# A backbone layer with sparse experts: row transposes of two experts together, one branch an expert, and the last experts' tokens finished in slot order

## The chip, the cores and the metric

One core of one Trainium2 chip runs the kernel. The metric is the device time of one execution in microseconds (us); lower is better.

## What is computed

One layer: a token mixer, then a mixture of experts, on 512 latent tokens of 1024 channels, all float32. The change touches the experts and the final norm alone. For each token the router picks one group of eight experts and in it two experts:

```python
top_logits, top_idx = lax.top_k(in_group, TOP_K)
weights = jax.nn.softmax(top_logits, axis=-1) * p_group
expert_id = g_idx * EXPERTS_PER_GROUP + top_idx
for e in range(N_EXPERTS):
    act = jax.nn.silu(h @ w_gate[e]) * (h @ w_up[e])
    out = out + gate[:, e:e + 1] * (act @ w_down[e])
x = x + gt2 * out.reshape(x.shape)
return rmsnorm(x, g_final)
```

There are 32 experts; each has gate and up matrices of 1024 x 256 and a down matrix of 256 x 1024, so 3 MB of weights. Both experts of a token are in the same group.

## The kernel before, in words

The mixer and the router end with tables: for each expert the list of its tokens (`ix`, and `ixh` for halves of rows), the number of its tokens as a class of size (`size`), and the two weights of each token (`pw`). Normalised tokens lie in DRAM (`h2d`), the residual stream too (`x1d`).

**The loop (L1632 to L1673)** has 33 rounds. In round e TensorE multiplies expert e by gate and up and expert e - 1 by down:
- `gather_e` (L1397): GpSimd reads the size into a register, walks a tree of branches and gathers up to 128 rows of `h2d` by an indirect DMA into one of two tiles `xg`.
- `tile_x` (L1329): eight transposes bring the rows to channel-major in PSUM; ScalarE and VectorE copy four each to `st`.
- `tile_gu` (L1347): gate and up for 64 tokens. Two column halves of the array work on gate and up. A second half (tokens 65 to 128) runs under a branch in `halves` (L1408).
- `tile_act` (L1352) and `tile_at` (L1358): silu and product, four transposes of 64 x 64 out of partitions 64 to 127, one copy to `at`.
- `tile_down` (L1367), again with a second half under a branch.
- `tile_y` (L1376): VectorE multiplies by the gate of the residual branch; `scatter_e` (L1415) writes half rows to `ybuf` in DRAM, the second half under a branch of GpSimd.

So TensorE meets two branches an expert, and one register load `load_wide` (L1613). On TensorE, ScalarE and VectorE the order is as written; on GpSimd and the DMA queue of SyncE a scheduler orders by when it takes an instruction to be ready. Weights come through a ring of 20 buffers (`eraw`, `part_load`), some six experts ahead.

**The end.** Tokens of experts 30 and 31 are not scattered: `last_prepare` and `last_turn` build one-hot matrices, `last_y` splits the results into a high and a low part, and `last_own` adds them to the sum in PSUM by matmuls (L1580), where `last_x` (L1575) has put the residual rows and `last_mix` (L1587) adds the scattered results that `last_rows` (L1564) loads. Sum of squares, square root, reciprocal and the last product follow for four tiles of 128 tokens; each is stored by a plain DMA.

Of the kernel before, what the change touches and what calls it, by code (L numbers as in the profile page):

```python
# [26 lines left out]
def hybrid_kernel(  # L27
# [8 lines left out]
    nc = tc.nc  # L36
# [1213 lines left out]
    for c_ in range(2):  # L1250
        gcopy(gt2h[64 * c_:64 * c_ + 64], gt2[64 * c_:64 * c_ + 64, 512 * c_:512 * c_ + 512])
        G.memset(cofs[64 * c_:64 * c_ + 64], float(c_))
    xgs = [mo.tile([128, D], F32, name=f"xg{j}", tag=f"xg{j}", bufs=1) for j in range(NXG)]
    for a_ in xgs:
        G.memset(a_, 0.0)

    pw = mz2.tile([128, NT, 2], F32, name="pw")

# [41 lines left out]
    ix = indices(pt[:, 0:2 * NE].rearrange("p (a e) -> p a e", a=2), 128, NE, "tb")  # L1300
    pcnt = ps_s5("pcnt")
# [14 lines left out]
    V.tensor_tensor_scan(cnt[:, 3], onesf1, cnt[:, 2], 0.0, op0=ALU.mult, op1=ALU.add)  # L1316
    ngen = mz2.tile([1, 1], I32, name="ngen")
# [11 lines left out]
    def tile_x(xg, st, h):  # L1329

        pt = ps_tp("pxt").rearrange("p (k s) -> p k s", k=4)
        for k in range(4):
            T.transpose(pt[:, k, :], xg[:, 4 * h + k:D:8], ident)  # L1333
        if h:
            V.tensor_copy(st[:, 4:8], pt)  # L1335
        else:
            S.activation(st[:, 0:4], pt, AF.Copy)

    def new_st():
        return mo.tile([128, KD, 128], F32, tag="st", name="st")  # L1340
# [6 lines left out]
    def tile_gu(pg, st, r, a):  # L1347
        for k in range(KD):
            for c in range(2):
                T.matmul(pg[H[c], 256 * a:256 * a + 256], lhsT=st[:, k, H[a]], rhs=r[c][k // 4][:, 256 * (k % 4):256 * (k % 4) + 256], start=(k == 0), stop=(k == KD - 1), skip_group_check=True)  # L1350

    def tile_act(pg):  # L1352
        sg = mo.tile([128, 512], F32, tag="sge", name="sge", bufs=2)
        S.activation(sg[64:128], pg[0:64], AF.Silu)
        V.tensor_tensor(sg[64:128], pg[64:128], sg[64:128], op=ALU.mult)
        return sg

    def tile_at(sg):  # L1358
# [37 lines left out]

    def gather_e(e):  # L1397
        if e < NE:
            more[e] = nc.values_load(size[0:1, e:e + 1], engines=[EN.Pool], min_val=0, max_val=len(SIZES) - 1, skip_runtime_bounds_check_because=BYC)
            by_size(e, lambda n: gather(xgs[e % NXG][0:n], ix[0:n, 0, e:e + 1]))  # L1400

    scattered = []

    def scatter_h(e, a, y):
        return G.indirect_dma_start(out=ybuf.rearrange("r (c n) -> (r c) n", c=2), out_offset=bass.IndirectOffsetOnAxis(ap=ixh[:, a, e:e + 1], axis=0),  # L1405
                                    in_=y[:, 512 * a:512 * a + 512], in_offset=None, bounds_check=4 * L - 1, oob_is_err=False)
# [15 lines left out]

    for e in range(NXG):
        gather_e(e)

# [3 lines left out]
    with tc.If(n_gen > 0):  # L1429
        with tc.For_i(0, n_gen, 1):  # L1430
            row = mz2.tile([1, 3, NE], F32, name="grow")
# [44 lines left out]
            xt_ = new_st().rearrange("p k s -> p (k s)")  # L1476
# [18 lines left out]
            pd = [ps_mm("ped0"), ps_mm("ped1")]  # L1495
            for k in range(2):
# [9 lines left out]
    x1s = []  # L1506

    def last_loads():
        for h in range(2):
            t = eraw("x1").rearrange("p (i d) -> p i d", i=2)  # L1510
            SY.dma_start(out=t, in_=x1d[256 * h:256 * h + 256].rearrange("(i p) d -> p i d", p=128))
            x1s.append(t)
        x1s.append(eraw("gfin")[:, 0:1024])
        SY.dma_start(out=x1s[2], in_=g_final.rearrange("(o d) -> o d", o=1).to_broadcast([128, D]))


    DIRECT = (NE - 2, NE - 1)
    last = {}

    sel = mz2.tile([128, 2, 2, NT, 2], F32, name="sel")  # L1520

    def last_weights():

        for j, e in enumerate(DIRECT):
            V.tensor_scalar(sel[:, j, 0], ex, float(e), None, op0=ALU.is_equal)
            V.tensor_tensor(sel[:, j, 1], sel[:, j, 0], pw, op=ALU.mult)
            V.tensor_tensor(sel[:, j, 1, :, 0], sel[:, j, 1, :, 0], sel[:, j, 1, :, 1], op=ALU.add)

    def last_prepare(j):

        g, t = (xgs[j][:, 512 * k:512 * k + 512].rearrange("p (i s) -> p i s", i=NT) for k in range(2))
        gtt(g, oh[:, :, 0, :], sel[:, j, 0, :, 0:1].to_broadcast([128, NT, 128]), ALU.mult)
        gtt(t, oh[:, :, 1, :], sel[:, j, 0, :, 1:2].to_broadcast([128, NT, 128]), ALU.mult)
        gtt(g, g, t, ALU.add)

    def last_turn(j):
        if j == 0:
            last["oh"] = eraw("loh").bitcast(F32R)
            last["gs"] = mz2.tile([128, 2], F32, name="gs")
        pt = ps_tp("pht")  # L1540
        for i in range(NT):
            T.transpose(pt[:, 128 * i:128 * i + 128], xgs[j][:, 128 * i:128 * i + 128], ident)
        S.activation(last["oh"][:, 512 * j:512 * j + 512], pt, AF.Copy)
        pg = ps_tp("pgs")
        for i in range(NT):
            T.matmul(pg[:, 0:1], lhsT=xgs[j][:, 128 * i:128 * i + 128], rhs=sel[:, j, 1, i, 0:1], start=(i == 0), stop=(i == NT - 1))  # L1546
        V.tensor_copy(last["gs"][:, j:j + 1], pg[:, 0:1])

    def last_y(pd, j):

        y, parts = new_y(), eraw("yp").bitcast(F32R)
        g_ = last["gs"][:, j:j + 1]
        for a in range(2):
            for c in range(2):
                V.tensor_tensor(y[H[a], 512 * c:512 * c + 512], pd[a][H[c]], gt2h[H[c]], op=ALU.mult)  # L1555
        hi, lo = parts[:, 0:1024], parts[:, 1024:2048]
        S.activation(hi, y, AF.Copy, scale=g_)
        V.scalar_tensor_tensor(lo, y, g_, hi.bitcast(F32), op0=ALU.mult, op1=ALU.subtract)
        return hi, lo

    ssf = mz2.tile([128, 4, NT], F32, name="ssf")
    yrs, xis, fin = [], [], {}

    def last_rows():  # L1564

        for i in range(NT):
            t = eraw("yr").rearrange("p (q d) -> p q d", q=2)
            yb = bass.AP(ybuf.tensor, ybuf.offset + 128 * i * D, [[D, 128], [L * D, 2], [1, D]])
            ld = SY.dma_start(out=t, in_=yb)
            for p_ in scattered:  # L1570
                tc.add_manual_dep(ld.ins if hasattr(ld, "ins") else ld, (p_.ins if hasattr(p_, "ins") else p_).name, mybir.DependencyInfo(mybir.DependencyClass.Sync, mybir.DependencyReason.DATA), reason="results of every expert")
# [146 lines left out]
```

## Time and profile before

| | us |
|---|---|
| runs shown | 882.38, 878.52, 880.90 |
| median | 880.9 |
| profiled execution | 880.24 |
| its span, first to last instruction | 878.5 |
| TensorE busy in the span | 738.2 (84%) |
| VectorE, ScalarE, GpSimd busy | 458.5, 321.2, 329.6 |

The span is what the trace covers; the profiled execution's own time lies 1.7 us above it. Busy shares are means over stages: the experts' loop fills the stretch from about 552 to 850 us, and the end follows it. In rows of the trace PE is TensorE's multiplier, PEld its weight load, DVE VectorE, ACT ScalarE, POOL GpSimd; a q behind a name is that engine's sequencer.

### The profile page before, as it was taken

How to read it: one execution, taken by the hardware profiler on the slowest of the kernel's cores; microseconds unless marked ns; L12 is line 12 of the kernel's file. 1: busy time of each engine (PE TensorE's matmuls, PEld its weight loads, DVE VectorE, ACT ScalarE, POOL GpSimd, SP SyncE). 2: the span in 40 equal slices, each digit the busy share in tenths (PEclk: the TensorE clock that was granted, in tenths of full speed). 3: DMA queues.
4: the chain of work that ended last, by engine and by line, in shares of the span. 5: the costliest groups of instructions: out<-in, count | busy, mean ns of one | idle time of the engine just before them, and what ended most of it. 6: DMA issues, size and time to landing. Idle time of an engine off the chain costs nothing. (4 is left out here: it accounts for less than half of the span.)

```text
span 878.5 us, 14308 instructions
## 1 busy us (share of the span) xinstructions
PE 738.2 (84%) x5486; PEld 513.4 (58%) x5486; DVE 458.5 (52%) x723; ACT 321.2 (37%) x559; POOL 329.6 (38%) x293
## 2 busy tenths in 40 slices
PE   3498986998978986979999993788998998888885
PEld 0376863665656775746778872455655655555542
DVE  3948565355397798725985576133223232332344
ACT  3442621355465748526632331221112112121133
POOL 4647435345486697621610122122122122221400
PEclk9998997999989999989999996899999999999999
DMA  8916870342145454478687437999989998998042
GB/s 308 272 47 194 196 230 22 106 126 73 48 140 174 150 177 130 137 241 322 202 297 274 156 121 314 394 392 398 381 304 388 406 360 332 387 397 295 18 192 95
DMA packets 84679, 202.01 MB, mean 230 GB/s; under 512 B 12860, under 2 KB 42622, under 8 KB 74867
## 3 DMA queue, kind: packets, MB, share of 16 engines
q1 hardware_dynamic: 76754, 180.00, 57.7%
q0 software_dynamic: 5856, 12.45, 4.0%
q10 hardware_dynamic: 1984, 8.44, 3.6%
q8 instruction: 53, 0.87, 0.4%
q14 instruction: 32, 0.25, 0.1%
HBM read 180.16 MB, written 26.69 MB: 235 GB/s over the span
## 5 line engine op out<-in xcount | busy, mean ns | idle before, releaser
L1350 PE MATMUL peg<-eraw,st 128*64 128x256 f32 x1152 | 132.8, 384 | 8.4 <-PEq L1411 6.8
L1350 PEld LDWEIGHTS peg<-eraw,st 128*64 128x64 f32 x1152 | 94.1, 138 | 58.8 <-issue 33.9
L1335 DVE COPY st<-pxt 128x512 f32<-128x512 f32 x32 | 22.1, 691 | 158.7 <-PE pxt L1333 158.7
L1364 ACT ACTIVATE at<-pat 128x256 f32<-128x256 f32 x32 | 12.3, 383 | 216.0 <-PE pat L1362 216.0
L1322 POOL DMA_INDIRECT xg<-h2d,tb x32 | 30.3, 948 | 141.3 <-PE pxt L1333 129.9
L396 PE MATMUL zp<-hh,zuwh 128*128 128x512 f32 x192 | 78.2, 407 | 0.0
L398 PE MATMUL zp<-hh,zuwl 128*128 128x512 f32 x192 | 76.2, 397 | 0.5 <-POOL zuwl L757 0.4
L397 PE MATMUL zp<-hl,zuwh 128*128 128x512 f32 x192 | 76.0, 396 | 0.0
L1370 PE MATMUL ped<-eraw,at 128*64 128x512 f32 x288 | 68.9, 603 | 0.0
L98 POOL TENSOR_TENSOR adacc<-adacc,wa 128x512 f32<-128x512 f32 x30 | 47.2, 1574 | 40.9 <-ACT wa L857 38.7
L1405 POOL DMA_INDIRECT ybuf<-ye,ixh x34 | 33.9, 996 | 69.2 <-DVE ye L1380 41.6
L1380 DVE TENSOR_TENSOR ye<-ped,gt2h 128x512 f32<-128x512 f32 x60 | 39.0, 686 | 39.7 <-PE ped L1370 38.5
L1333 PE MATMUL pxt<-ident,xg 128*128 128x128 f32 x256 | 42.3, 303 | 8.5 <-DMA xg<-h2d,tb 7.7
L396 PEld LDWEIGHTS zp<-hh,zuwh 128*128 128x128 f32 x192 | 36.9, 192 | 11.7 <-issue 4.4
L398 PEld LDWEIGHTS zp<-hh,zuwl 128*128 128x128 f32 x192 | 36.7, 191 | 9.8 <-POOL zuwl L757 1.8
L1333 PEld LDWEIGHTS pxt<-ident,xg 128*128 128x128 f32 x256 | 33.6, 194 | 13.5 <-issue 9.0
L397 PEld LDWEIGHTS zp<-hl,zuwh 128*128 128x128 f32 x192 | 36.8, 192 | 7.1
L1362 PE MATMUL pat<-ident,sge 64*128 64x64 f32 x128 | 21.3, 286 | 19.0 <-PEq L1411 18.3
L1362 PEld LDWEIGHTS pat<-ident,sge 64*128 64x128 f32 x128 | 17.7, 209 | 32.8 <-PEq L1411 30.5
L1370 PEld LDWEIGHTS ped<-eraw,at 128*64 128x64 f32 x288 | 17.8, 136 | 27.2 <-issue 23.6
L98 POOL TENSOR_TENSOR vb<-vta,vtb 128x512 f32<-128x512 f32 x16 | 21.9, 1366 | 31.3 <-PE pv L533 20.2
L757 DVE TENSOR_TENSOR zuwl<-zr,zuwh 128x1024 fp32r<-128x1024 f32 x16 | 28.4, 1778 | 4.6 <-ACT zuwh L756 4.5
(499 smaller groups left out, 1652.7 us busy)
## 6 DMA issues: line engine op xcount, KB each, us to landing
eraw<-in_w_exp_gate_dram SPq DMA_DIRECT2D x24, 1024.0 KB
eraw<-in_w_exp_up_dram SPq DMA_DIRECT2D x24, 1024.0 KB
eraw<-in_w_exp_down_dram SPq DMA_DIRECT2D x24, 1024.0 KB
wa<-in_w_ada_dram SPq DMA_DIRECT2D x32, 512.0 KB
zr<-in_w_in_dram SPq DMA_DIRECT2D x12, 1024.0 KB
wa<-in_w_ada_dram SPq DMA_DIRECT2D x8, 1024.0 KB
eraw<-in_w_exp_gate_dram SPq DMA_DIRECT2D x14, 512.0 KB
eraw<-in_w_exp_down_dram SPq DMA_DIRECT2D x14, 512.0 KB
```

The costliest lines, as they stand in the source:

```text
L98: G.tensor_tensor(o, a, b, op=op)
L396: T.matmul(acc, lhsT=wh, rhs=ah, start=start, stop=False)
L397: T.matmul(acc, lhsT=wh, rhs=al, start=False, stop=False)
L398: T.matmul(acc, lhsT=wl, rhs=ah, start=False, stop=stop)
L757: (G if t in ZPOOL else V).tensor_tensor(zu[t][1], raw, zu[t][0].bitcast(F32), op=ALU.subtract)
L1322: G.indirect_dma_start(out=xg, out_offset=None, in_=h2d, in_offset=bass.IndirectOffsetOnAxis(ap=idx, axis=0), bounds_check=L - 1, oob_is_e ...
L1333: T.transpose(pt[:, k, :], xg[:, 4 * h + k:D:8], ident)
L1350: T.matmul(pg[H[c], 256 * a:256 * a + 256], lhsT=st[:, k, H[a]], rhs=r[c][k // 4][:, 256 * (k % 4):256 * (k % 4) + 256], start=(k == 0), s ...
L1362: T.transpose(pa[:, 128 * k + 64 * a:128 * k + 64 * a + 64], sg[64:128, 256 * a + k:256 * a + 256:2], ident[64:128, 64:128])
L1370: T.matmul(pd[a][H[c]], lhsT=at[:, 128 * k + 64 * a:128 * k + 64 * a + 64], rhs=r[2][k][:, 512 * c:512 * c + 512], start=(k == 0), stop=(k ...
L1380: V.tensor_tensor(y[:, 512 * a:512 * a + 512], pd[a], gt2h, op=ALU.mult)
L1405: return G.indirect_dma_start(out=ybuf.rearrange("r (c n) -> (r c) n", c=2), out_offset=bass.IndirectOffsetOnAxis(ap=ixh[:, a, e:e + 1], a ...
```

## The change

- **Rows.** Two experts share one tile: the even one's rows in partitions 0 to 63, the odd one's in 64 to 127 (`xgs`, now three). Eight transposes turn both, and the copies go back into the same tile (`turn`, `turned`). Rows 65 to 128 of an expert go to tiles of their own (`xws`, two), gathered and turned only where an expert has over 64 tokens.
- **Activations.** The product is written by two VectorE operations so that its even columns lie in partitions 0 to 63 and its odd ones in 64 to 127; the four transposes use two row tiles and two PSUM tiles, copied by ScalarE and VectorE.
- **One branch.** Down of e - 1 and gate/up of e for tokens over 64, and the turn of the next pair's second tile, stand in one block (`second`), entered if a count `some[e]` is over zero; inside, two more tests choose.
- **Order of the experts.** The last expert of each group (7, 15, 23, 31) comes at the end (`ORD`). No token has two of these four.
- **The end.** Tokens of those four stay in slot order: residual rows, weights and the other expert's result are gathered by GpSimd (`own_rows`, `own_other`), summed by VectorE (`own_base`, `own_sum`), normalised and scattered to the output (`own_out`). All others are finished in four tiles as before, without TensorE, and scattered to the output with an index that drops the others' rows (`last_out`).

```diff
+    DIR = tuple(range(EPG - 1, NE, EPG))
+    ORD = [x_ for x_ in range(NE) if x_ not in DIR] + list(DIR)
...
+    xgs = [mo.tile([128, D], F32, name=f"xg{j}", tag=f"xg{j}", bufs=1) for j in range(3)]
+    xws = [mo.tile([128, D], F32, name=f"xw{j}", tag=f"xw{j}", bufs=1) for j in range(2)]
...
+    def turn(xg, pts):
+        for h in range(2):
+            for k in range(4):
+                T.transpose(pts[h][:, 128 * k:128 * k + 128], xg[:, 4 * h + k:D:8], ident)
+    def turned(xg, pts):
+        S.activation(xg[:, 0:512], pts[0], AF.Copy)
+        V.tensor_copy(xg[:, 512:1024], pts[1])
...
-        V.tensor_tensor(sg[64:128], pg[64:128], sg[64:128], op=ALU.mult)
+        for k in range(2):
+            V.tensor_tensor(sg[H[k], k:512:2], pg[64:128, k:512:2], sg[64:128, k:512:2], op=ALU.mult)
...
+        for a in range(2):
+            for k in range(2):
+                T.transpose(pas[k][:, 64 * a:64 * a + 64], sg[H[k], 256 * a + k:256 * a + 256:2], ident[H[k], H[k]])
-        S.activation(at, pa, AF.Copy)
+        S.activation(at[:, 0:128], pas[0][:, 0:128], AF.Copy)
+        V.tensor_copy(at[:, 128:256], pas[1][:, 0:128])
...
+    def own_get(src, dst, k, j, rows):
+        def one(a):
+            return G.indirect_dma_start(out=dst[:, a], out_offset=None, in_=src, in_offset=bass.IndirectOffsetOnAxis(ap=own["ix"][:, k, a, j:j + 1], axis=0),
+                                        bounds_check=rows - 1, oob_is_err=False)
+        return halves(own["n"][j], one)
+    def own_alloc():
...
+        for nm in ("b", "y"):
+            for i in range(2):
+                t = eraw("own" + nm)
+                G.memset(t, 0.0)
...
+    def own_rows(j):
+        own_get(half_rows(x1d), own["b"][j], 1, j, 2 * L)
+        own_get(pwd, own["w"][:, j], 0, j, 4 * L)
+    def own_other(j):
+        for ld in own_get(half_rows(ybuf), own["y"][j], 2, j, 4 * L):
+            after_all(ld)
+    def own_base(j):
+        for a in range(2):
+            b = own["b"][j][:, a]
+            V.scalar_tensor_tensor(b, own["y"][j][:, a], own["w"][:, j, a, 1:2], b, op0=ALU.mult, op1=ALU.add)
+    def own_sum(j, pd):
+        for a in range(2):
+            b, t = own["b"][j][:, a], own["y"][j][:, a]
+            V.scalar_tensor_tensor(t, pd[a], own["w"][:, j, a, 0:1], gt2h, op0=ALU.mult, op1=ALU.mult)
+            V.tensor_tensor(b, b, t, op=ALU.add)
+        for a in range(2):
+            S.activation(own["y"][j][:, a], own["b"][j][:, a], AF.Square, accum_out=ssf[:, 0, DC[j] + a:DC[j] + a + 1])
...
+    def second(e, last, gu, nxt):
+        t = nc.values_load(some[0:1, e:e + 1], engines=[EN.PE], min_val=0, max_val=4, skip_runtime_bounds_check_because=BYC)
+        with tc.If(t > 0):
+            for x_, f in ((e - 1, last), (e, gu)):
+                if f:
+                    with tc.If(load_size(x_, EN.PE) > SIZES.index(64)):
+                        f()
+            if nxt:
+                nxt()
...
         for e in range(NE + 1):
-            gather_e(e + NXG)
+            gather_e(e + 4)
             if e > 0:
                 sg = tile_act(pgs[(e - 1) % 2])
             if e < NE:
-                halves(wide[e], lambda a: tile_gu(pgs[e % 2], st[e], eraws[e], a))
+                tile_gu(pgs[e % 2], e, eraws[e], 0)
+            if e in (NE - 2, NE - 1):
+                for i in (0, 1) if e == NE - 2 else (2, 3):
+                    last_scale(i)
+                    last_mix(i)
+            if e == NE - 1:
+                for i in (0, 1):
+                    last_sum(i)
             if e == NE:
+                recip(0)
+                for i in (0, 1):
+                    last_out(i)
+                for j in (0, 1):
+                    own_out(j)
             if e > 0:
                 at = tile_at(sg)
+            if e == NE - 1:
+                roots(0)
+                last_sum(2)
...
+            nxt = e % 2 == 1 and e + 2 < NE
+            p_ = (e + 1) // 2
+            if nxt:
+                turn(xgs[p_ % 3], pts)
+                turned(xgs[p_ % 3], pts)
             if e > 0:
-                halves(wide[e - 1], lambda a: tile_down(pd, at, eraws[e - 1], a))
+                tile_down(pd, at, eraws[e - 1], 0)
+            second(e, (lambda: tile_down(pd, at, eraws[e - 1], 1)) if e > 0 else None,
+                   (lambda: tile_gu(pgs[e % 2], e, eraws[e], 1)) if e < NE else None,
+                   (lambda: turn(xws[p_ % 2], pts)) if nxt else None)
+            if nxt:
+                turned(xws[p_ % 2], pts)
+            if 0 < e <= NE - ND:
                 scatter_e(e - 1, tile_y(pd))
+            if e > NE - ND:
+                if e < NE:
+                    own_base(e - 1 - NE + ND)
+                own_sum(e - 1 - NE + ND, pd)
+                if e == NE - 1:
+                    own_base(ND - 1)
+            gather_w(e + 3)
...
+            if e == NE - 5:
+                own_alloc()
+                for j in range(ND):
+                    own_rows(j)
+            if e == NE - 4:
                 last_rows()
+                for j in range(ND):
+                    own_other(j)
```

`last_tables` fills the new index tables in round 1 with some 20 small VectorE operations in place of six; `some` is filled with the other tables, ahead of the loop. What follows the loop is now a last reciprocal, two tiles' output, and the outputs of the third and fourth direct expert.

## Rows read from the trace of the kernel before

**Rows 1.** Table of stretches: us, busy by engine (count), clock, DMA share, GB/s.
```profile
720.00:800.00 80.00, 70.55 (x498) 44.64 (x496) 26.05 (x39) 14.12 (x27) 20.37 (x21) 1.00 0.98 373
...
812.00:836.00 24.00, 21.38 (x152) 13.31 (x150) 8.02 (x12) 4.15 (x8) 10.55 (x10) 1.00 0.05 17
```

**Rows 2.** TensorE's timeline over one expert: start, duration, engine, line, operation, idle before.
```profile
806.11 3.67 PE L1350 MATMUL peg<-eraw,st 128*64 128x256 f32 x32 [0.31 <-PEq L1411]
810.48 0.66 PE L1362 MATMUL pat<-ident,sge 64*128 64x64 f32 x4 [0.70 <-PEq L1411]
811.07 1.31 PE L1333 MATMUL pxt<-ident,xg 128*128 128x128 f32 x8
812.32 1.94 PE L1370 MATMUL ped<-eraw,at 128*64 128x512 f32 x8
814.56 0.65 PE L1350 MATMUL peg<-eraw,st 128*64 128x256 f32 x4 [0.31 <-PEq L1411]
```

**Rows 3.** Branch line's records, 809 to 815: duration min/median/max, first and last start.
```profile
L1411 PEldq EVENT_SEMAPHORE  x2: 51/51/51, 809.8 to 814.3; - x2
L1411 PEldq COMPARE_BRANCH  x1: 202/202/202, 811.7 to 811.7; - x1
```

**Rows 4.** The register load of the size, same stretch and columns.
```profile
L1615 PEldq TENSOR_LOAD <-size x1: 300/300/300, 810.0 to 810.0; - x1
```

**Rows 5.** TensorE's timeline, experts of over 64 tokens: gate/up, then down.
```profile
621.10 7.13 PE L1350 MATMUL peg<-eraw,st 128*64 128x256 f32 x64 [0.31 <-PEq L1411]
...
641.17 3.65 PE L1370 MATMUL ped<-eraw,at 128*64 128x512 f32 x16
```

**Rows 6.** Timeline of all engines at the loop's start.
```profile
546.10 0.99 POOL L1322 DMA_INDIRECT xg<-h2d,tb  x1 [8.46 <-DVE tb L1283]
...
547.39 0.92 POOL L1322 DMA_INDIRECT xg<-h2d,tb  x1 [0.30 <-issue]
...
552.40 1.94 PE L1333 MATMUL pxt<-ident,xg 128*128 128x128 f32 x8 [7.65 <-DMA xg<-h2d,tb]
...
561.78 3.67 PE L1350 MATMUL peg<-eraw,st 128*64 128x256 f32 x32 [0.30 <-ACT st L1337]
...
573.69 0.69 DVE L1355 TENSOR_TENSOR sge<-peg,sge 64x512 f32<-64x512 f32 x1 [0.16 <-ACT sge L1354]
```

**Rows 7.** Groups by line, 545 us to the end: count, busy us, mean ns, idle before.
```profile
L1354 ACT ACTIVATE sge<-peg 64x512 f32<-64x512 f32 x32 | 18.8, 588 | 0.7
L1364 ACT ACTIVATE at<-pat 128x256 f32<-128x256 f32 x32 | 12.3, 383 | 216.0 <-PE pat L1362 216.0
...
L1590 DVE SCALAR_TENSOR_TENSOR yr<-yr,pw 128x1024 f32<-128x1024 f32 x4 | 5.0, 1279 | 1.3 <-ACT yr L1589 1.3
L1589 ACT ACTIVATE yr<-yr,pw 128x1024 f32<-128x1024 f32 x4 | 4.4, 1136 | 0.0
...
L1354 ACT ACT_TABLE_LOAD x2 | 2.6, 1283 | 0.0
...
L1596 ACT ACTIVATE yr<-fin 128x512 f32<-128x512 f32 x4 | 2.4, 591 | 4.8 <-PE fin L1592 4.7
...
L1607 DVE SCALAR_TENSOR_TENSOR x<-fin,ssf,gfin 128x512 f32<-128x512 f32 x2 | 1.4, 748 | 0.0
```

**Rows 8.** The branch line's records on GpSimd's sequencer, whole span, columns of rows 3.
```profile
L1411 POOLq INC_SWDGE_SEM  x26: 540/1282/1740, 571.0 to 832.2; - x26
```

**Rows 9.** The memsets of the row tiles on GpSimd, columns of rows 3.
```profile
L1255 POOL MEMSET xg<- x2: 956/958/961, 535.8 to 536.7; 128x1024 f32 x2
```

**Rows 10.** GpSimd's timeline in round 29: mask products, then expert 28's scatter.
```profile
820.93 2.05 POOL L98 TENSOR_TENSOR xg<-oh,sel 128x512 f32<-128x512 bf16 x2 [4.66 <-PE pxt L1333]
...
824.48 1.01 POOL L1405 DMA_INDIRECT ybuf<-ye,ixh  x1 [0.15 <-issue]
```

**Rows 11.** The scatters of line 1405, from issue to landing.
```profile
DMA to landing us min/median/max: 2.3/7.2/9.3
```

**Rows 12.** The stores of the output on SyncE's queue, columns of rows 3.
```profile
L1608 SPq DMA_DIRECT2D out_dram<-x x2: 332/332/333, 871.6 to 874.6; - x2
```

More of the change, by code (lines that the diff above doesn't have):

```diff
@@ L1421, in scatter_e @@
         scattered.extend(ins)
-    for e in range(NXG):
+    for e in range(4):
         gather_e(e)
+    for e in range(3):
+        gather_w(e)
     itr = mz2.tile([1, 4], F32, name="itr")
@@ L1504, in hybrid_kernel, with ins_of, after_all @@
             V.tensor_scalar(itr[:, 0:1], itr[:, 0:1], 1.0, None, op0=ALU.add)
-    x1s = []
+    own = {}
+    x1s, yrs, ids = [], [], {}
+    ssf = mz2.tile([128, 2, 12], F32, name="ssf")
+    GRP = ((0, 6), (6, 10), (10, 12))
+    BC = (0, 1, 6, 7)
+    DC = (2, 4, 8, 10)
+    def ins_of(i):
+        return i.ins if hasattr(i, "ins") else i
+    def after_all(ld):
+        for p_ in scattered:
+            tc.add_manual_dep(ins_of(ld), ins_of(p_).name, mybir.DependencyInfo(mybir.DependencyClass.Sync, mybir.DependencyReason.DATA), reason="results of every expert")
@@ L1529, in last_prepare @@
[L1529 to L1547, printed above, removed]
@@ new lines, in roots, with recip, no_order @@
+    def roots(g):
+        lo, hi = GRP[g]
+        d = slice(hi - (4 if g == 0 else 2), hi)
+        for c in range(2):
+            V.tensor_copy(ssf[H[c], 1, d], ssf[H[1 - c], 0, d])
+        V.tensor_tensor(ssf[:, 0, d], ssf[:, 0, d], ssf[:, 1, d], op=ALU.add)
+        S.activation(ssf[:, 1, lo:hi], ssf[:, 0, lo:hi], AF.Sqrt, bias=eps, scale=1.0 / D)
+    def recip(g):
+        lo, hi = GRP[g]
+        V.reciprocal(ssf[:, 1, lo:hi], ssf[:, 1, lo:hi])
+    stored = []
+    def no_order(ins):
+        for i_ in ins:
+            for p_ in stored:
+                tc.declare_no_dep(ins_of(i_), ins_of(p_), reason="rows of different tokens")
+        stored.extend(ins)
@@ new lines, in own_out, with one @@
+    def own_out(j):
+        b = own["b"][j]
+        for a in range(2):
+            V.scalar_tensor_tensor(b[:, a], b[:, a], ssf[:, 1, DC[j] + a:DC[j] + a + 1], own["gfh"], op0=ALU.mult, op1=ALU.mult)
+        def one(a):
+            return G.indirect_dma_start(out=half_rows(out[0]), out_offset=bass.IndirectOffsetOnAxis(ap=own["ix"][:, 1, a, j:j + 1], axis=0), in_=b[:, a], in_offset=None,
+                                        bounds_check=2 * L - 1, oob_is_err=False)
+        no_order(halves(own["n"][j], one))
@@ L1568, in last_rows @@
             yb = bass.AP(ybuf.tensor, ybuf.offset + 128 * i * D, [[D, 128], [L * D, 2], [1, D]])
[L1569 to L1571 removed]
+            after_all(SY.dma_start(out=t, in_=yb))
             yrs.append(t)
[L1573 removed]
@@ L1575, in last_x, with last_scale @@
-    def last_x(i):
-        for h in range(2):
-            T.matmul(fin[i][h], lhsT=ident, rhs=xis[i][:, 512 * h:512 * h + 512], start=True, stop=False, skip_group_check=True)
-    def last_own(j, parts):
-        for i in range(NT):
-            for r_ in parts:
-                for h in range(2):
-                    T.matmul(fin[i][h], lhsT=last["oh"][:, 512 * j + 128 * i:512 * j + 128 * i + 128], rhs=r_[:, 512 * h:512 * h + 512], start=False, stop=False, skip_group_check=True)
+    def last_scale(i):
+        S.activation(yrs[i][:, 0], yrs[i][:, 0], AF.Copy, scale=pw[:, i, 0:1])
@@ L1623, in hybrid_kernel @@
             V.memset(t, 0.0)
-        load_wide(0)
-        st[0] = new_st()
-        for h in range(2):
-            tile_x(xgs[0], st[0], h)
+        for xs_ in (xgs, xws):
+            turn(xs_[0], pts)
+            turned(xs_[0], pts)
         for m in range(13, 17):
```

204 lines of the change are left out of this document (99 added, 105 removed).

## The prediction

> **What bounds the kernel now.** I read the table of stretches first, then TensorE's timeline over one expert, then the sequencer's records in it, and last GpSimd and the DMA landings. From 720 to 800 us TensorE is busy 70.6 of 80 us at full clock while the DMA share is 0.98 [rows 1]: both look full, and the timeline decides. One expert takes 8.45 us, from its gate/up matmuls at 806.11 to the next at 814.56 [rows 2]: gate/up 3.67, idle 0.70, four activation transposes 0.66 (the next starts after 0.59), eight row transposes 1.31 (1.25), down 1.94, idle 0.31. No gap is a wait for weights; both are put down to the branch line. So TensorE in its own order is the bound, and the weights arrive earlier than needed.
>
> The two idles are not the branch: its compare runs at 811.7, long before the gap. It is the skipped path's semaphore event, which goes out when the matmuls before it have drained (809.8 and 814.3) [rows 3]; a drain with restart costs 0.31, and the 0.70 holds a register load of 0.30, issued after it at 810.0 [rows 4]. A path that is taken costs no idle: an expert of over 64 tokens runs both gate/up halves in 7.13, so 3.46 for the second, and both down halves in 3.65, so 1.71 [rows 5]. The timeline shows this pattern twice, four such experts in all: 8, 9, 14 and 15. In the changed order they are numbers 7, 8, 13 and 29.
>
> **The sum, start.** The first row transposes ran at 552.40, 6.3 after their gather was issued; they will wait for the second expert's gather, issued at 547.39, so 553.7 [rows 6]. Then 1.94 for the transposes, some 0.8 for the copies in place, 1.94 for the second tile's transposes (which nobody needs yet), gate/up 0 at 4.4 (3.67 warm, with a part at the lower clock level) and one drain with its load 0.70: gate/up 1 at about 563.4, against 561.78, so +1.6 (0 to +4). The new tables put some 14 more small VectorE operations after expert 0's eviction, about 0.17 each, ahead of the product that started at 573.69 with almost no slack [rows 6]: +2.3, once.
>
> **The loop.** *Odd numbers:* gate/up 3.67, activation transposes 0.55, row transposes 1.25, down 1.94, one drain 0.31: 7.7. *Even numbers* have no row transposes, so down has nothing in front of it while the transposed activations are copied: ACT's 256 columns took 0.383 [rows 7] and VectorE's 512 took 0.69 [rows 6], so 128 columns are about 0.3, with hand-over 0.45; sum 6.9. The drain after gate/up goes, as does the load behind it; the new load stands ahead of the branch and runs while TensorE still works, so I cost it at nothing; without that cover it is 0.40. The second half of the product (two operations for one) lies beside 3.67 of gate/up.
>
> For four transposes on two row tiles no row here gives a time: 0.66 if nothing changes [rows 2], half of it at best; 0.55 is near the only row. The Trainium skill (TensorE: Matmul & The Clock Gate, Part 3) says that matmuls on different row groups run at once; by that rule they take 0.33.
>
> Extras: in ten numbers the one branch is taken (5, 7, 8, 9, 11, 13, 14, 27, 29, 30), since the test also looks at the next pair. Second halves as in [rows 5]; seven turns of the second tile at 1.31; and where both inner tests fail (5, 11, 27), a second skip with its load after the drain, 1.15. Up to number 27 that is 26.5: 2.46 each for 5, 11 and 27, 4.77 for 7 and 13, 4.86 for 8, 3.0 for 9, 1.71 for 14.
>
> From gate/up 1 to gate/up 28: 14 odd at 7.7, 13 even at 6.9, 26.5: 224.0, against 806.11 - 561.78 = 244.3. With the start, gate/up 28 comes at 561.8 + 3.9 + 224.0 = 789.7, **16.4 earlier**. Weights allow it: the DMA engines have next to nothing to do from 812 on [rows 1].
>
> **The end.** From gate/up 28 to the end it was 72.4 (806.11 to 878.5). Now everything hangs on expert 27's scatter, which all final loads wait for. Its down ends at 789.7 + 6.6 = 796.3, evicted 1 later: 797.3. But GpSimd, between there and the two experts before, gets eight gathers at 1.0, each with a skipped branch whose semaphore record takes 0.54 to 1.74 [rows 8], and four memsets of 2048 columns at 1.92, twice the 0.958 of 1024 [rows 9]; with 0.5 beyond the gather it overlaps and 0.3 for the test, 1.8 each, and 1.0 for expert 15's second halves: 23 us, for which it has about 3.6 idle. The order on GpSimd is not the written one: the mask products, written after a scatter, ran at 820.93 ahead of it at 824.48 [rows 10]. So some of the 23 will be done sooner; I take half, scatter at 804.5. Landing took 2.3 at least and 7.2 in the median [rows 11]: 4.5 after its end, at 810. GpSimd then gathers the other results: 1.0, landing 5.5: 816.4. SyncE's loads of the scattered results wait for the same scatter and take 2.8 a tile at the 373 GB/s of [rows 1], so 813 to 821, ahead of their scales; residual rows and gains, moved ahead on that queue, lie behind the last weights and are there by then.
>
> VectorE has by then stood 7 us at the base of the first direct expert, with the product of expert 29 queued behind it, and TensorE behind that. From 816.4, with 0.75 and 0.69 for 512 columns, 1.28 for 1024, 1.13 for a scale, 0.8 for a sum of squares over 512 with its read and 1.3 over 1024, 0.59 for silu, 1.28 for a table load [rows 6, 7]:
> - base and sum 4.3, second square 0.8, silu 0.59, product 0.86: 822.9;
> - two scales and mixes and the copy, 3.1 (GpSimd's additions of the mixed tiles lie beside the 13 until their squares); then down 29 in two halves and a drain, 4.0: gate/up 31 at 830.0;
> - sum 2.9; then on ACT a square 0.8, silu 0.59, two scales 2.26, two sums of squares 2.6, the copy 0.28: down 30 at 839.1;
> - down 1.94, sum 2.9, square 0.8, a table load 1.28 (square roots now come ahead of the last silu), silu and product 1.45: 847.4;
> - VectorE has two outputs of 1.28 and four of 0.75 ahead of its half of the copy: down 31 at 853.4;
> - down 1.94, sum 2.9, two outputs 2.56, roots and reciprocals 0.8, two and one outputs 2.25: 863.9; scatter 1.05, landing 3.5 (the last store was issued at 874.6, the end 878.5 [rows 12]): **868.4**.
>
> So the end grows from 72.4 to 78.7 and the loop gives 16.4: 10.1 less. The profiled execution had 880.24 for a span of 878.5, 1.7 around it; so 870.1. The median of the runs shown, 880.9, is 0.66 above that execution: **870.8**. A measurement tells about 0.5% from no change: 876.5 to 885.3.
>
> **Rivals.**
> 1. *GpSimd is out of the way:* the scheduler has placed memsets and gathers in idle time, scatter at 797: by the same sum 7 less, 864. For: GpSimd is busy 20.4 of 80 us [rows 1]. Against: the buffers come free only with numbers 26 and 27. Chance 0.17.
> 2. *GpSimd stands in front of the scatter with all 23 us,* as written: scatter at 816.5, other rows 828.5, the same chain 12 later: 883, no change. If each skip takes the record's median 1.28 beyond the gather, 8 more in both groups: 891, **slower**. It decides at a scatter later than about 819. For: the text has them ahead of it. Against: the mask products moved. Chance 0.20 (0.12 and 0.08).
> 3. *The load before the branch is not hidden:* 0.40 in each of some 22 skips, 8.8: 879.6, no change. Against: the compare that ran 2.6 before the drain. Chance 0.10.
> 4. *The row tiles run fully side by side:* 0.22 less in 27 numbers, 6: 865. The rule named above says so; no row here shows two row tiles. Chance 0.06.
> 5. *Skipping a longer block stalls on its instructions:* the two skips become one of up to 96 instructions, against 64 now (32 matmuls and their weight loads for gate/up; 8 and theirs for down, 8 and theirs for the turn), which cost the plain gaps of [rows 2]. If a third of 23 skips had to fetch, at a landing of 6.3 [rows 6] less the 2.6 of lead, 30 more: 900, slower. The Trainium skill (Runtime: NRT & Kernel Launch, Instruction fetch mechanics) says that a branch out of the fetched window waits for a DMA; the skips here show no such wait. Chance 0.04.
>
> **How the numbers follow.** Forecast 0.43 (its own range 866 to 876: 4 each way for the start and the row tiles). Faster: 0.40 of it, rival 1's 0.17, 0.05 of rival 4: 0.62. Same: 0.03 of the forecast, 0.12 of rival 2, 0.06 of rival 3, 0.01 of rival 4: 0.22. Slower: 0.08 of rival 2, 0.04 of rival 3 (with a longer wait of the copies in the even numbers), rival 5: 0.16. The range reaches from rival 1 with its start bound, 860, to rival 2 between its two prices, 887.
>
> **What would show it.** Gate/up starts 6.9 and 7.7 apart in turn; no idle after gate/up; 0.31 after down in skipped numbers; gate/up 28 near 790. On GpSimd the memsets and gathers ahead of the last scatter; VectorE idle some 7 us before the first base; TensorE idle 10 us before down 29. If gate/up 28 comes later than 798, the loop's sum is wrong; if the base waits over 12 us, rival 2 holds.

## The result and the profile after

| | before | after |
|---|---|---|
| runs, us | 878.52 to 882.38 (4) | 900.40 to 905.64 (4) |
| median, us | 880.38 | 901.50 |
| profiled execution / span, us | 880.24 / 878.5 | 905.64 / 903.9 |

After over before is 1.0263, with a 95% interval of 1.0219 to 1.0307: **slower by 2.6%**, where 870.8 us and a gain were forecast. (The ratio also counts two further executions of the changed kernel, 904.11 and 908.33.) The profiled execution lies 4.1 above its median.

Below, number n is the expert at place n of the order that a kernel works in, counted from 0; gate/up n and down n are its matmuls, and "number n takes" is the time from gate/up n to gate/up n + 1. Kernel n is the kernel of experiment n. A base is the sum of an expert's residual rows and the other experts' results for them (`own_base`).

The table of stretches, columns of [rows 1]: the loop, the last experts, the end.

```profile
720.00:800.00 80.00, 73.16 (x536) 44.14 (x532) 34.42 (x66) 16.11 (x33) 21.43 (x22) 1.00 1.02 382
812.00:836.00 24.00, 11.79 (x94) 7.59 (x92) 1.68 (x3) 1.47 (x3) 10.65 (x11) 0.87 0.88 330
850.00:903.00 53.00, 14.72 (x66) 4.94 (x62) 34.95 (x50) 17.13 (x33) 19.31 (x12) 0.60 0.11 40
```

From 720 to 800 TensorE is fuller than in [rows 1], 73.2 us instead of 70.6. From 812 to 836 it is busy half the time, VectorE and ScalarE next to nothing: all wait. The loop is better and the end worse.

TensorE's timeline over one pair of numbers, against [rows 2]:

```profile
721.14 3.67 PE L1370 MATMUL peg<-eraw,xg 128*64 128x256 f32 x32 [0.36 <-PEq L1708]
724.74 0.45 PE L1383 MATMUL pat<-ident,sge 64*128 64x64 f32 x4
725.12 1.16 PE L1354 MATMUL pxt<-ident,xg 128*128 128x128 f32 x8
726.21 1.94 PE L1392 MATMUL ped<-eraw,at 128*64 128x512 f32 x8
728.61 3.67 PE L1370 MATMUL peg<-eraw,xg 128*64 128x256 f32 x32 [0.46 <-PE ped L1392]
732.21 0.45 PE L1383 MATMUL pat<-ident,sge 64*128 64x64 f32 x4
733.08 1.94 PE L1392 MATMUL ped<-eraw,at 128*64 128x512 f32 x8 [0.41 <-ACT at L1385]
735.41 3.67 PE L1370 MATMUL peg<-eraw,xg 128*64 128x256 f32 x32 [0.40 <-PEq L1708]
```

An odd number takes 7.47, an even one 6.80; 7.7 and 6.9 were forecast. The 0.70 behind gate/up is gone, one drain of 0.31 to 0.46 is left. The row transposes begin 0.38 after the activation transposes, not 0.59. So the 21 us more come from elsewhere: from the start, from single numbers, and most of all from the end. Three places show where.

**The start** (timelines of VectorE, GpSimd and TensorE):

```profile
536.60 4.67 DVE L1176 TENSOR_SCALAR rsc<-io,rsc 128x4 f32<-128x4 f32 x1
536.70 2.75 POOL L1260 MEMSET xg<- 128x1024 f32 x3
536.73 4.54 DVE L1172 MAX8 mxs<-lgs 128x8 f32<-128x8 f32 x1
539.38 1.86 POOL L1260 MEMSET xw<- 128x1024 f32 x2
...
549.45 1.00 POOL L1343 DMA_INDIRECT xg<-h2d,tb  x1 [8.21 <-DVE some L1337]
551.38 0.92 POOL L1343 DMA_INDIRECT xg<-h2d,tb  x1 [0.93 <-issue]
557.71 1.94 PE L1354 MATMUL pxt<-ident,xg 128*128 128x128 f32 x8 [9.61 <-DMA xg<-h2d,tb]
559.72 1.28 ACT L1358 ACT_TABLE_LOAD   x1 [24.60 <-issue]
```

Two small VectorE operations of the router end at 541.27, the moment GpSimd has cleared its fifth tile. In the kernel before, beside two clears, the first of them is:

```profile
536.37 1.29 DVE L1170 TENSOR_SCALAR rsc<-io,rsc 128x4 f32<-128x4 f32 x1
```

The first gather is 3.35 later than in [rows 6], the second another 0.64, because a test now stands between them; a table load of 1.28 stands in front of the first copy. Of the 3.35, 0.95 is not the change's: this execution reached the router's last norm that much later (534.59 instead of 533.64). From the norm to the first gather it is 14.9 instead of 12.5.

**Number 5** (GpSimd's timeline, then TensorE's):

```profile
596.23 1.05 POOL L1608 DMA_INDIRECT lw<-pwd,lix  x1 [6.40 <-DMA pwd<-pwt]
...
603.72 1.00 POOL L1608 DMA_INDIRECT lw<-pwd,lix  x1 [0.31 <-issue]
605.03 0.95 POOL L1343 DMA_INDIRECT xg<-h2d,tb  x1 [0.30 <-issue]
...
607.54 0.95 POOL L1343 DMA_INDIRECT xw<-h2d,ixw  x1 [0.30 <-issue]
...
602.30 3.67 PE L1370 MATMUL peg<-eraw,xg 128*64 128x256 f32 x32 [0.31 <-PEq L1708]
...
613.14 3.68 PE L1392 MATMUL ped<-eraw,at 128*64 128x512 f32 x8 [5.69 <-ACT at L1385]
618.14 1.94 PE L1354 MATMUL pxt<-ident,xw 128*128 128x128 f32 x8 [1.32 <-PEq L1711]
```

The token weights that `own_rows` gathers are written 25 rounds later; on GpSimd they stand behind the scatter of number 1 at 588.83, the second in the trace (the expectation of experiment 2 calls it the third). The first waits 6.40 for its table, and the rows of the next pairs queue behind all five. Gate/up 6 comes at 620.02, 17.7 after gate/up 5, where 10.2 (7.7 and 2.46 extra) was forecast.

**The end** (GpSimd, VectorE):

```profile
813.84 1.03 POOL L1440 DMA_INDIRECT ybuf<-ye,ixh  x1 [0.30 <-issue]
821.94 1.03 POOL L1608 DMA_INDIRECT owny<-ybuf,lix  x1 [7.07 <-DMA ybuf<-ye,ixh]
...
832.08 1.83 POOL L1620 MEMSET ownb<- 128x2048 f32 x1
834.18 1.01 POOL L1608 DMA_INDIRECT ownb<-x1d,lix  x1 [0.27 <-POOL ownb L1620]
...
838.40 1.42 DVE L1637 SCALAR_TENSOR_TENSOR ownb<-owny,lw,ownb 128x512 f32<-128x512 f32 x2 [16.55 <-DMA ownb<-x1d,lix]
...
846.53 6.07 POOL L98 TENSOR_TENSOR eraw<-eraw,yr 128x1024 f32<-128x1024 f32 x2 [8.73 <-DVE yr L1692]
847.88 5.28 DVE L1637 SCALAR_TENSOR_TENSOR ownb<-owny,lw,ownb 128x512 f32<-128x512 f32 x2
...
890.68 0.98 POOL L1675 DMA_INDIRECT out_dram<-ownb,lix  x1 [0.31 <-issue]
```

Expert 27's scatter is issued at 813.84. The first base on VectorE runs at 838.40, 24.6 later, after a wait of 16.55 that ends with the residual rows. Their buffer is cleared last of the four. The next two rows stand side by side: while GpSimd adds, two VectorE operations take 5.28 instead of 1.42. The row below is GpSimd's at the closing line of the program, columns of [rows 3]:

```profile
L1830 POOLq DRAIN  x3: 46/99/8644, 894.5 to 903.7; - x3
```

From 893.5 on the DMA engines move nothing more; GpSimd drains for 8.64 us, and the program waits for that.

### The profile page after: what moved, and what is told of

It is laid out like the page before. It is cut to its first block, busy times and chain, and to the rows that moved or that the text cites. A ratio compares the mean times of both kernels' runs of the same rounds, so it can differ in the third digit from the quotient of the medians.

```text
span 903.9 us, 14338 instructions
## 1 busy us (share of the span) xinstructions
PE 708.6 (78%) x5334; PEld 484.4 (54%) x5334; DVE 497.3 (55%) x824; ACT 321.4 (36%) x564; POOL 370.2 (41%) x323
## 5 line engine op out<-in xcount | busy, mean ns | idle before, releaser
L1370 PE MATMUL peg<-eraw,xg 128*64 128x256 f32 x1024 | 120.0, 386 | 8.8 <-PEq L1708 6.9
L1370 PEld LDWEIGHTS peg<-eraw,xg 128*64 128x64 f32 x1024 | 81.3, 139 | 54.7 <-issue 28.7
L1392 PE MATMUL ped<-eraw,at 128*64 128x512 f32 x288 | 77.4, 666 | 18.4 <-ACT at L1385 15.5
L1385 ACT ACTIVATE at<-pat 128x128 f32<-128x128 f32 x32 | 8.8, 276 | 109.4 <-PE pat L1383 57.5
L1383 PE MATMUL pat<-ident,sge 64*128 64x64 f32 x128 | 16.2, 309 | 34.2 <-DVE sge L1377 34.2
L1386 DVE COPY at<-pat 128x128 f32<-128x128 f32 x32 | 9.3, 292 | 59.0 <-PE pat L1383 48.9
L1359 DVE COPY xw<-pxt 128x512 f32<-128x512 f32 x16 | 11.1, 692 | 51.8 <-PE pxt L1354 34.8
L1383 PEld LDWEIGHTS pat<-ident,sge 64*128 64x128 f32 x128 | 11.0, 202 | 48.8 <-DVE sge L1377 36.7
L1377 DVE TENSOR_TENSOR sge<-peg,sge 64x256 f32<-64x256 f32 x64 | 27.4, 428 | 14.5 <-ACT sge L1375 12.7
L1375 ACT ACTIVATE sge<-peg 64x512 f32<-64x512 f32 x32 | 18.9, 590 | 39.9 <-PEq L1708 28.5
```

Of the source, the lines that this page charges most:

```text
L1370: T.matmul(pg[H[c], 256 * a:256 * a + 256], lhsT=st[:, k, H[e % 2]], rhs=r[c][k // 4][:, 256 * (k % 4):256 * (k % 4) + 256], start=(k == 0 ...
L1377: V.tensor_tensor(sg[H[k], k:512:2], pg[64:128, k:512:2], sg[64:128, k:512:2], op=ALU.mult)
L1383: T.transpose(pas[k][:, 64 * a:64 * a + 64], sg[H[k], 256 * a + k:256 * a + 256:2], ident[H[k], H[k]])
L1392: T.matmul(pd[a][H[c]], lhsT=at[:, 128 * k + 64 * a:128 * k + 64 * a + 64], rhs=r[2][k][:, 512 * c:512 * c + 512], start=(k == 0), stop=(k ...
```

## The experiments

The theory behind the runs: the loop gains as forecast; the start, the early gathers and the end lose it. The rival: the loop itself waits for rows, and the end only passes that on.

**1. The loop without the new end.**

```diff
-    ORD = [x_ for x_ in range(NE) if x_ not in DIR] + list(DIR)
+    ORD = list(range(NE))
...
+                fin[0], fin[1], fin[2] = pas, pgs, pts
```

The functions of the end are those of the kernel before; its sums use the banks that the loop leaves free.

> The changed loop (two experts' rows in one tile, row tiles, one branch) with the order of the experts and the end of the kernel before. Theory (the loop gains, the new end and the early GpSimd gathers lose): gate/up 1 still near 569, no stall between numbers 5 and 6, gate/up 28 at 788 to 792, then 72 to the end: 861 to 866 us. Rival (the loop itself gains nothing, because turning two experts together waits for rows): gate/up 28 at 800 or later, 873 us or more.

Measured 870.4 us, ratio 0.988 (0.982 to 0.993); gate/up 28 at 799.05, then 71.9 to the end. That is between the theory and the rival: the new end costs more than the loop gains, but the loop gains less than expected. Numbers 13 and 19 take 14.7 and 11.2. There VectorE cannot write its result (GpSimd's timeline, then VectorE's):

```profile
657.95 0.97 POOL L1438 DMA_INDIRECT ybuf<-ye,ixh  x1 [0.30 <-issue]
666.79 0.97 POOL L1438 DMA_INDIRECT ybuf<-ye,ixh  x1 [7.87 <-issue]
...
673.28 1.02 POOL L1438 DMA_INDIRECT ybuf<-ye,ixh  x1 [0.30 <-issue]
...
674.21 1.29 DVE L1400 TENSOR_TENSOR ye<-ped,gt2h 128x512 f32<-128x512 f32 x2 [7.25 <-DMA ybuf<-ye,ixh]
```

**2. The token weights gathered later.**

```diff
-        own_get(pwd, own["w"][:, j], 0, j, 4 * L)
+        for ld in own_get(pwd, own["w"][:, j], 0, j, 4 * L):
+            p_ = scattered[2 * (14 + 3 * j)]
+            tc.add_manual_dep(ins_of(ld), ins_of(p_).name, ...)
```

> The changed kernel, but the gathers of the direct experts' token weights stand behind the scatters of numbers 14, 17, 20 and 23 instead of behind the third scatter. Theory (they stand in front of the rows of pair 6 and 7 on GpSimd and cost the stall between numbers 5 and 6): gate/up 6 near 610 instead of 620.0, everything behind it 9 to 10 earlier, 891 to 893 us. Rival (the stall is the landing of the rows themselves, with three buffers for the pairs): gate/up 6 stays at 618 or later, 899 us or more.

Gate/up 6 at 611.30, 9.4 after gate/up 5: the stall is gone, as the theory says. The total, 904.0 us, did not fall. The gathers waited in their new place: the edit has them wait for a scatter to land, and GpSimd stood 6.8 us at 711 (the trace names a weight load as what ended it). VectorE and TensorE waited behind them, and number 18 took 13.7 instead of 6.8: the expected total missed because of my own wait.

**3. Residual rows first.**

```diff
-        own_get(half_rows(x1d), own["b"][j], 1, j, 2 * L)
+        own["r"].extend(own_get(half_rows(x1d), own["b"][j], 1, j, 2 * L))
...
             after_all(ld)
+            for p_ in own["r"]:
+                tc.add_manual_dep(ins_of(ld), ins_of(p_).name, ...)
```

> The changed kernel, but on GpSimd the residual rows of the direct experts (and the clearing of their buffer) stand before the gathers of the other results, in the time in which GpSimd waits for the last scatter. Theory (the first base waits for the residual rows because they come last on GpSimd): first base at 832 to 834 instead of 838.4, end 4 to 6 earlier, 896 to 898 us. Rival (the base waits for the landing of the other results behind the loads of the scattered rows): base at 837 or later, within 2 of 901.5 us.

The dependency orders the two on GpSimd and waits for nothing. 894.2 us; this execution began its loop 5.5 earlier, so differences count:

```profile
805.92 1.02 POOL L1440 DMA_INDIRECT ybuf<-ye,ixh  x1 [0.31 <-issue]
...
813.93 1.00 POOL L1608 DMA_INDIRECT owny<-ybuf,lix  x1 [1.23 <-DMA ybuf<-ye,ixh]
819.08 1.00 POOL L1608 DMA_INDIRECT owny<-ybuf,lix  x1 [4.15 <-DMA xg<-h2d,tb]
...
825.36 1.42 DVE L1639 SCALAR_TENSOR_TENSOR ownb<-owny,lw,ownb 128x512 f32<-128x512 f32 x2 [11.51 <-DMA owny<-ybuf,lix]
```

From the last scatter to the first base it is 19.4 instead of 24.6, and from the base to the end 65.5 as in the changed kernel. The place of the residual rows cost 5.1. What the base waits for now is the landing of the other results, as the rival has it. Between the first and the second gather lie two skipped tests of 1.9 each.

**4. Plain stores.**

```diff
-            return G.indirect_dma_start(out=half_rows(out[0]), ...
+            return SY.dma_start(out=od[256 * j + 128 * a:256 * j + 128 * a + 128], in_=b[:, a])
...
-        no_order([G.indirect_dma_start(out=out[0], ...
+        no_order([SY.dma_start(out=out[0, 128 * i:128 * i + 128], in_=x1s[i])])
```

> The changed kernel with all final stores as plain DMAs of SyncE: the four tiles to the output by rows, the direct experts' rows to a scratch tensor, so the direct experts' tokens are left out of the output. Theory (the last 8.6 us are GpSimd's drain after its own DMAs, all of whose data has landed): no drain over 1 us at the end, last store to end 3.5 to 4.5 instead of 13.2, 889 to 893 us. Rival (the stores' landing is slow because 512 rows are stored at once): last store to end 8 or more, 897 us or more.

894.9 us, a little over the theory's 889 to 893; span 891.5, the last store issued at 888.46: 3.0 to the end. GpSimd's drain is still there, and longer, but it begins at 859.3, beside other work (4.4 of it beside GpSimd's own last addition):

```profile
L1830 POOLq DRAIN  x3: 46/105/12413, 859.3 to 891.2; - x3
```

From gate/up 30 to the end it is 74.0 instead of 82.9. The drain costs only where it ends last.

**5. Second halves free,** on kernel 1.

```diff
-        for i_ in ins:
-            for p_ in scattered:
+        for k_, i_ in enumerate(ins):
+            for p_ in scattered + ins[:k_]:
                 tc.declare_no_dep(...)
```

> The first experiment's kernel (changed loop, old end), but the scatter of an expert's second half no longer waits until its first half has landed. Theory (GpSimd stands 7 to 9 us at that wait after each expert of over 64 tokens, the next scatters come late, VectorE waits for a free result buffer and TensorE behind it): numbers 13 and 19 take 9 and 7.5 us instead of 14.7 and 11.2, total 861 to 863 us. Rival (two result buffers are too few for a landing of 7 to 9 us, whatever the order): VectorE still waits for the scatters, 867 us or more.

866.2 us, ratio 0.985 (0.981 to 0.988), between theory and rival; the profiled execution has 862.9. Numbers 13 and 19 take 9.4 and 7.5, and VectorE no longer waits for a scatter anywhere. The waits in front of line 1438 on GpSimd's sequencer, first of kernel 1:

```profile
L1438 POOLq EVENT_SEMAPHORE  x34: 17/17/9367, 574.8 to 816.5; - x34
```

and of this kernel:

```profile
L1438 POOLq EVENT_SEMAPHORE  x34: 17/17/17, 571.8 to 806.3; - x34
```

The kernel before has the same ordered halves; GpSimd waited there too (three times, 19.6 us), but no VectorE operation waited for it.

**6. Tiles cleared later,** on kernel 5.

```diff
-    for a_ in xgs + xws:
-        G.memset(a_, 0.0)
+    G.memset(xgs[0], 0.0)
...
+    for a_ in (xws[0], xgs[1], xws[1], xgs[2]):
+        behind(G.memset(a_, 0.0), g1)
```

> The kernel of the experiment before (second halves free), but of the five cleared row tiles only one is cleared before the first gather, the other four behind the second, and the first two gathers stand next to each other. Theory (clearing five tiles on GpSimd holds up VectorE in the router, where two operations took 4.6 us, and the test between the gathers costs 0.6): those two VectorE operations below 1.5 us, first row transposes 3.5 to 4.5 earlier against the end of the router's norm, total 3 to 4 less than the experiment before. Rival (the router's operations wait for something else): they stay at 4 us or more and nothing is gained.

856.6 us, 9.6 less by the medians and 8.7 by the profiled executions, where 3 to 4 was expected. The two operations of the router:

```profile
533.50 1.23 DVE L1176 TENSOR_SCALAR rsc<-io,rsc 128x4 f32<-128x4 f32 x1
533.63 1.10 DVE L1172 MAX8 mxs<-lgs 128x8 f32<-128x8 f32 x1
```

From the router's norm (531.62) to the first gather (542.91) it is 11.3 instead of 14.9, from first to second gather 0.6 less: the 4 of the theory. The rows also landed 3.2 sooner after the second gather, which nothing here explains and which kernel 7 does not repeat.

**7. Weights and tables early,** on kernel 6.

```diff
+        weights()
+        last_weights()
         turn(xgs[0], pts)
         turned(xgs[0], pts)
...
+            if e == 0:
+                turn(xws[0], pts)
```

> The kernel of the experiment before, and also: token weights and their tables computed while VectorE waits for the first gather, not after expert 0; the first turn of the second tile behind gate/up 0. Theory: number 2 takes 7 us instead of 9.6, the table load leaves the path ahead of gate/up 0, total 3 to 5 less than the experiment before, 852 to 856 us. Rival (these lie beside other waits): less than 1.5 gained.

**855.0 us, ratio 0.969 (0.964 to 0.974): the fastest kernel,** but only 1.6 below the one before it, with runs that overlap (849.1 to 856.1, and 854.2 to 860.4): the theory's 3 to 5 does not show in the total. Number 2 takes 6.7, as expected, and from the first turn to gate/up 1 it is 9.5 instead of 11.9; its start came later in this execution. From gate/up 1 (562.76) to gate/up 28 (782.88) it is 220.1, against 244.3 in [rows 2, 6].

**8. Additions on VectorE,** in the changed kernel.

```diff
-        gtt(x1s[i], x1s[i], y, ALU.add)
+        V.tensor_tensor(x1s[i], x1s[i], y, op=ALU.add)
```

> The changed kernel, but the four additions of the scattered rows to the residual rows run on VectorE instead of GpSimd. Theory (while GpSimd adds, a VectorE operation of 0.7 or 0.25 us takes up to 4 longer, on the path): VectorE's base and copies at their usual times, from the first base to the last store 2 to 5 less although VectorE has four operations of 1.3 more, total 896 to 900 us. Rival (VectorE waits for something else there): 4 to 6 more on VectorE, 903 us or more.

901.9 us. The long operations are gone:

```profile
844.40 1.40 DVE L1637 SCALAR_TENSOR_TENSOR ownb<-owny,lw,ownb 128x512 f32<-128x512 f32 x2
```

But from the first base (832.41) to the last store (884.78) it is 52.4, as before (52.3). The four additions of 1.23 and VectorE's waits for TensorE took the place of what was gained: the slow operations are shown, a cost of them on the path is not.

**9. The new end with everything mended** (edits 2, 3, 5, 6, 7 together; the gathers of 2 only put behind, without a wait).

> The changed kernel with its end, and all that the other runs mended: token weights gathered later, residual rows first, second halves free, four tiles cleared behind the first gathers, tables computed while VectorE waits for the rows. Theory (the new end itself is some 25 longer than the old one: GpSimd's gathers, its drain and a chain through VectorE): gate/up 28 at 780 to 785, from there 95 to 98 to the end instead of 72 with the old end, 877 to 884 us, no change against the kernel before. Rival (the new end only suffers from the stalls ahead of it): 75 to 85 from gate/up 28 to the end, 860 to 870 us.

886.6 us, ratio 1.007 (1.004 to 1.009). Gate/up 28 at 784.58, then 100.8: over the theory's 95 to 98, far from the rival's 75 to 85. With kernel 7's old end it was 71.5. The 29 between them is not all the end's: some 5 is the second halves of number 29, which in kernel 7's order lie ahead of gate/up 28. And one stall is left ahead of it: number 27 takes 14.1 instead of 9.2, because gate/up 27 waits for weights, which in no other kernel costs it over 0.3:

```profile
773.59 5.35 PE L1369 MATMUL peg<-eraw,xg 128*64 128x256 f32 x30 [2.49 <-DMA eraw<-in_w_exp_up_dram]
```

From gate/up 1 to the end, where the order doesn't matter, it is 322.5 against 291.6: the new end with its order of experts costs 31 us, up to 5 of them in number 27.

**10 and 11. Something on GpSimd at the very end,** on kernel 7.

```diff
-        SY.dma_start(out=out[0, 128 * i:128 * i + 128], in_=xi)
+        (G if i == NT - 1 else SY).dma_start(out=out[0, 128 * i:128 * i + 128], in_=xi)
```

```diff
+        if i == NT - 1:
+            gcopy(ssf[:, 0, 0:1], xi[:, 0:1])
```

> The fastest kernel so far (changed loop, old end, all mended), but the last of its four stores is issued by GpSimd, as a plain DMA. Theory (GpSimd drains for 6 to 9 us when its last work is done, and only the end of the program shows it): a drain of 6 to 9 behind that store, 4 to 6 more in the span than with SyncE's store, whose landing alone took 3. Rival (only indirect DMAs make the drain): drain below 1, span within 2.

> The same fastest kernel, with one operation of one column on GpSimd behind the last product of VectorE, no DMA. Theory (the drain follows GpSimd's last work of any kind): a drain of 6 to 9 us behind it, 4 to 6 more in the span. Rival (only its DMAs make the drain): drain below 1 or long over by then, span within 2.

One execution each. Spans 855.1 and 856.7, drains of 7.65 and 7.19 at the end. Kernel 11's operation and its drain:

```profile
848.74 0.19 POOL L101 TENSOR_SCALAR ssf<-x 128x1 f32<-128x1 f32 x1 [43.93 <-DVE x L1655]
```

```profile
L1774 POOLq DRAIN  x3: 46/109/7189, 848.7 to 856.5; - x3
```

From the end of VectorE's last product it is 8.7 and 7.5 to the end of the program; in kernel 7, with SyncE's store, 3.9. One small operation is enough. Since each execution starts its end at another time, the spans alone (0.7 and 2.3 more than kernel 7) would not have shown it.

## Why the prediction was wrong

By its own points, in the profiled execution:

| step | forecast | measured | difference |
|---|---|---|---|
| gate/up 1 | 563.4 | 569.09 | +5.7 |
| from there to gate/up 28 | 226.3 | 232.6 | +6.3 |
| from there to expert 27's scatter | 14.8 | 12.1 | -2.7 |
| from there to the first base | 11.9 | 24.6 | +12.7 |
| from there to the last store | 47.5 | 52.3 | +4.8 |
| from there to the end | 4.5 | 13.2 | +8.7 |

The sum is 35.5: 903.9 instead of 868.4. The step that failed is the end: from the last scatter on, 63.9 was forecast and 90.1 was measured. The sum gave GpSimd's work there too little time behind the scatter and none after the last store, and kernel 9, with the rest mended, still needs 100.8 from gate/up 28 where 78.7 was forecast. The start and number 5 come on top.

- **The loop was right.** 7.7 and 6.9 were 7.47 and 6.80; in kernel 9, with the same order of experts, gate/up 1 to 28 takes 221.7 (562.93 to 784.58), where 224.0 without the tables was forecast; without the wait in number 27 it would be 5 less, so the sum is some 7 too long. "No idle after gate/up, 0.31 after down" holds. Rival 3 falls: in the rows of the pair the drain shows 0.36 to 0.46, in other numbers 0.31, so at most 0.15 of the load's 0.40. Rival 5 falls: no skip of the one branch costs more. The four transposes on row tiles save 0.21 (the next start comes after 0.38 instead of 0.59). The Trainium skill (TensorE: Matmul & The Clock Gate, Part 3) has tiles of different row groups run at once, which would be half of 0.59; the 0.38 lies between. So rival 4 has most of its 0.22: 0.17 under the 0.55 of the sum. The row transposes took 1.09 to the next start instead of 1.25; why is open.
- **"If gate/up 28 comes later than 798, the loop's sum is wrong":** it came at 801.70, and the sum of its steps was still right. What failed is what I left out around them. At the start the new tiles' clearing had no term, since GpSimd was idle: an operation of VectorE's router took 3.4 longer, and from the norm to the first gather it is 2.4 more (kernel 6, with one tile cleared there instead of five, gets 3.6 back). Nor had the test between the gathers (0.6) and the table load (1.3). From the norm to gate/up 1 it is 28.1 in the kernel before, 34.5 here, and 32.9 to 34.5 in kernels 1 to 5 and 8, with the same start. The norm's own time wanders by 5 between executions; 0.95 of the 5.7 is that. The Trainium skill (SBUF — State Buffer, SBUF: two separate sides) says that VectorE and GpSimd share a pair of ports, which GpSimd or a VectorE operation in a two-port mode, as tensor_scalar can be, holds for a whole operation while the other stands still. The trace agrees, and is worse: a tensor_scalar of VectorE (4.67 here, 0.21 at 542.39) got no turn between five operations of GpSimd in a row.
- **The tables** cost 4.9 (number 2 takes 11.6, and 6.7 in kernel 7), not 2.3. The added operations were counted rightly: 20 (579.45 to 582.74) in place of six, so 14 more. What had no term is that the six already stick out of a shorter round: in kernel 1, which has only those, number 2 takes 9.6, and the added ones cost the other 2.0. TensorE, kept waiting 3.0 for the product, ran down 1 at a lower clock (granted 0.60; 3.19 instead of 1.94).
- **Number 5:** 7.6 that no step had. I let the scheduler of GpSimd place gathers early where that helped (half of the 23 us), and never asked what an early gather would wait for, and what stands behind it. Kernel 2 shows that these gathers are the cause: without them in this place number 5 takes 9.4, and in kernels 3, 4 and 8, where they stand as here, 14.8 to 16.5. In kernels 3 and 4 TensorE waits 6.8 and 6.0 for rows that are gathered behind them; in kernel 3:

```profile
610.67 1.94 PE L1354 MATMUL pxt<-ident,xw 128*128 128x128 f32 x8 [6.81 <-DMA xw<-h2d,ixw]
```

In this execution, as in kernel 8, most of the wait stands earlier, 5.7 in front of down 4, with a releaser that the trace doesn't show. Number 5 and number 2 together are 9.9 over; the other numbers up to gate/up 28 came 3.6 under their sum.
- **The end, +12.7:** "half, scatter at 804.5" was 2.7 too long for the scatter, but the other half did not vanish: it stood behind it. The base also waits for the residual rows, which I took to be there. Kernel 3 gives 5.1 for their place. Its rows hold the rest: 5.2 from the first gather of the other results to the second, after whose landing the base starts (6.3 later), and 8.0 instead of 5.5 from the scatter to the first. The 5.2 are a gather and two skipped tests, and a skipped test was priced at 0.5 beyond its gather: [rows 8] has 0.54 to 1.74 for the whole span, but here, near the end, it takes 1.98. "If the base waits over 12 us, rival 2 holds": it waited 16.6. Rival 2 had the right mechanism, too much work on GpSimd around the last scatter, with its place behind the scatter instead of in front.
- **Base to last store, +4.8:** down 30 and 31 ran at the lower clock after TensorE's waits (3.68 instead of 1.94 for the eight matmuls of down 30, at a granted clock of 0.50), and GpSimd's additions stretched VectorE's operations; kernel 8 leaves open how much of it each took.
- **The last term, +8.7:** I took 3.5 for the landing of the last store from a kernel that ends on SyncE. GpSimd's drain is in that kernel too, 6.6 us from 833.9, under other work. In the sum it had no term:

```profile
L1713 POOLq DRAIN  x3: 46/103/6606, 833.9 to 878.3; - x3
```

In front of the changed kernel's drain stands one more skipped test, 2.24 from 892.2; it had no term either.
- **Sums of the prediction that don't add up:** the step to down 30 comes to 839.4, not 839.1; the scatter at 804.5 lies 7.2 behind 797.3, where half of the 23 us less the 3.6 idle would be 7.9; rival 5's fetches come to 28, not 30. None of them changes the account.

## What to carry over

Price a stage that moves to GpSimd with its tail: its queue runs in the scheduler's order, each test between DMAs costs a record, each dependent step a landing, and here the program waited 7 to 9 us after its last operation, so let another engine finish. Before costing idle-time work at nothing, look at what the other engine on its port does at that moment. And a part of a change can be right while its companion sinks it: here the loop alone, with three waits mended, gives 3% where the whole change lost 2.6%.

## What the runs showed of the hardware

- GpSimd's closing drain takes 6.6 to 8.6 us after its last work, be it indirect DMAs, a plain DMA or one operation on one column (in kernel 4 it shows 12.4, 4.4 of them beside a running addition). In the changed kernel and kernels 2, 3, 8 and 9, which all end on GpSimd's scatters, it is 8.64 each time, whenever it starts (875.9 to 894.5).
- A run of five clears on GpSimd held two small VectorE operations for 4.5 us, the whole run of them; two clears held them for 1.2 in the kernel before.
- The record of a skipped indirect DMA grows along the program: 0.46 us at 549, 1.82 at 797, 2.24 at 892 in the changed kernel. Why is open; one near the end costs as much as two gathers. The test lines of `gather_w` and `halves`, columns of [rows 3]:

```profile
L1434 POOLq INC_SWDGE_SEM  x28: 461/1260/1815, 549.4 to 797.2; - x28
...
L1446 POOLq INC_SWDGE_SEM  x37: 613/1557/2240, 577.9 to 892.2; - x37
```
